# One decoder layer with block-sparse attention and a routed feed-forward: the attention loop issued in source order, and a new order at the start of the last stage

## The chip, the cores and the metric

The kernel runs on one core of one Trainium2 chip. That core has five engines with a queue of instructions each: TensorE (PE: matmuls and transposes; its weight loads are listed as PEld), VectorE (DVE), ScalarE (ACT), GpSimd (POOL) and SyncE (SP, which here only issues DMAs). The metric is the device time of one execution in microseconds, lower is better.

## The reference, cut to what matters

One layer works on h with 1024 tokens of width 1024:

```python
hn = rmsnorm(h)
z  = hn @ w_in                                   # u, v | q | six k/v groups | gates
oa = gelu(u) * (tril(w_s) @ rmsnorm(gelu(v)) + b_s)      # per chunk of 128 tokens
ob = g0*softmax(q kc^T) vc + g1*softmax(q ks^T) vs + g2*softmax(q kw^T) vw
h += concat(rmsnorm(oa), rmsnorm(ob)) @ w_o
h += hier_moe(rmsnorm(h))                        # 16 experts, 2 a token, of one group
h += (p @ w_ple_proj) * sigmoid(rmsnorm(h) @ w_ple_gate)
out = rmsnorm(h)
```

The attention has 8 heads in 2 groups. For the 1024 tokens of this case there are 16 blocks of 64 keys and 16 are selected, so the second branch sees all earlier keys; the third sees the last 512. Everything is float32; the kernel splits most operands into a high and a low part (`hi`, `lo`) and makes three matmuls of each product.

## The kernel before, in words

**Stages.** (1) Normalization and z = hn @ w_in, by column chunks (`z_chunk`). (2) The attention, a generator (`attention`) that walks through 132 slots. (3) `tail`: the last block of tokens, the router. (4) `moe`: 17 fixed blocks of rows with streamed expert weights, and three conditional groups of further blocks. (5) `ple`: gate, projection and the final norm, for eight tiles of 128 rows.

**The attention's slots.** The query blocks are walked in the order 1, 2, 3, 4, 0, 5, 6, 7 (`BLOCKS`). A unit is one block, one head group and one branch; its keys come in chunks of up to 512. A slot is one block of 128 keys of one unit, with 4 heads at once. In slot s the source writes down, in this order: the transposes of the probabilities of slot s+1 (`trans`, L644), their copy `ph` on ACT (L650); what was put off to this slot (`later`, run by `run_later`: exponentials L580, scale factors, copies); `pl` on DVE (L652); the output transposes of a finished group (`out`); steps of the query preparation (`prep`); a number of steps of `work`; the score matmuls of up to two banks into PSUM tiles `S`, of which there are two (L565), each with its maximum on DVE (L570); and the two products with V of slot s (`mult`, L669 and L670). POOL scales the probabilities (L604).

**The filler, `work`.** A second generator gives one matmul a step. In the first part (`z_prod`, tile `u`) it makes the last four row tiles of u, in two pairs of 2 x 24 matmuls, at no fewer than 7 a slot. Behind each pair, in the same step and without a yield, stand the evacuation of both tiles (`evac_u`: L232 on ACT, L244 and L247 on POOL, L245 and L248 on DVE, L246 and L252 on ACT, `rstd` L95 and L96 and L254 on POOL, the store L255 on POOL's queue) and the loading of output weights (`load_wo`: a DMA L745 issued by SP, the high part L748 on POOL, the low part L749 on DVE). Behind the first pair two weight chunks are loaded (2 and 3), behind the second, through `open_late`, four (4 to 7), then `gmoe` and `rt`. The staging tiles of chunks 4 to 7, `hT` and `hg`, have one buffer each. The second part of `work` multiplies by w_o (`prod`, L771), adds to h (`add`), transposes h for the router (`trans_h`) and computes its logits.

The core of the evacuation, one of two tiles whose closures run in the order written:

```python
nc.gpsimd.tensor_tensor(e, x, x, op=OP.mult)
nc.vector.scalar_tensor_tensor(e, e, 1 / 0.044715, x, op0=OP.add, op1=OP.mult)
nc.scalar.activation(e, e, AF.Tanh, scale=math.sqrt(2 / math.pi) * 0.044715)
nc.gpsimd.tensor_tensor(x, x, X[1], op=OP.mult)
nc.vector.scalar_tensor_tensor(x, e, 1.0, x, op0=OP.add, op1=OP.mult)
...
for k in (a, e, b, c, f, d, g, h):
    k()
```

**What sets the order.** Up to and with the attention loop a planner at compile time orders each engine's instructions by priority and by its own estimate of when operands are there; the steps of `work` have low priority there and may not go ahead of the slot's transposes (`issue_after`). From `manual_schedule` on (L1100) each engine gets its instructions in the order in which the source issues them; before, that holds from `tail` on.

**The start of the last stage.** `ple` loads h of tile 0 on SP, and on POOL's queue the two gathered expert outputs of tile 0 (`load_y(0)`, tiles `yg`, L1663), then h and `yg` of tile 1, h of tile 2 and `gf`. `proj(q)` makes a projection of four matmul instructions (L1741); `part(c)` splits one of eight gate weight chunks (ACT L1727, DVE L1728); `add_y(0)` adds the expert outputs (L1671); `trans` and `parts` prepare tile 0 for the gate matmuls (`mult`). The rows that are gathered come from `y_scr`, to which the last MoE block is written at L1613.

Of the kernel before, what the change touches and what calls it, by code (L numbers as in the profile page):

```python
# [8 lines left out]
F32 = mybir.dt.float32  # L9
# [4 lines left out]
AF = mybir.ActivationFunctionType  # L14
# [5 lines left out]
T = 1024  # L20
# [3 lines left out]
NP = 7  # L24
# [48 lines left out]
class K:  # L73
# [328 lines left out]
    def attention(self, blocks, done, work, count):  # L402
# [301 lines left out]
        for s in range(len(slots)):  # L704
            self.now = s
            lo = trans(s + 1) if s + 1 < len(slots) else None
            self.run_later()
            if lo:
                lo()
            for _ in range(min(2, len(self.pq))):  # L710
                self.pq.pop(0)()
            for _ in range(2 - bool(self.pq)):
                for i in [i for i in blocks if at[i] < len(STEPS)][:2]:
                    if start[first[i]] + STEPS[at[i]] - 0 <= s and may_step(i):
                        step(i)
                        break
            left = max(count[0] / (len(slots) - s), 0 if self.late else 7)
            n = 0
            with self.tc.high_priority(offset=-100000), self.tc.issue_after(anchor[0].ins):
                while n < left:  # L720
                    if next(work, None) is None:
                        break
                    count[0] -= 1
                    n += 1
            for n in range(2):
                b = state["bank"]
                if b < len(banks) and (n == 0 or due[b] + 0 <= s) and has_room(banks[b][0]) and may_score(b, due[b] <= s):
                    score()
            evac = mult(s)
            if s == len(slots) - 8:  # L730
                self.ple_load()
# [44 lines left out]
    def work(self, W, blocks):  # L776
# [25 lines left out]
        def load_h(X):  # L802
            X["h1"] = sb.tile([128, T], F32, name="h1", bufs=1)
            nc.sync.dma_start(X["h1"], self.A["x"][0, X["rows"]])
# [20 lines left out]
                nc.sync.dma_start(self.hg_scr[X["rows"]], X["hg"])  # L825

        def rest(X, nxt):
            trans_h(X, 1)
            load_h(nxt)
            self.logits(X["i"], X["hT"], X["hg"][:, T:T + 1])  # L830

        for i, X in M.items():
            X["i"] = i
# [6 lines left out]
        for n, i in enumerate(blocks[:-1]):  # L840
            X, N = M[i], M[blocks[n + 1]]
            X["sq"] = self.small.tile([128, 4], F32, name="sq")

            for t in range(NS + NF + n, NB, len(blocks) - 1):
                nc.sync.dma_start(self.y_scr[t * 128:(t + 1) * 128].rearrange("p (a n) -> p a n", a=2),
                                  X["oa"].unsqueeze(1).to_broadcast([128, 2, 512]))
            load_oa(N)
            while not i in self.ready:
                yield None
            X["ob"] = self.ready[i]  # L850
            trans(X, "ob")
            p = [None, None]
            for k in range(2):
                p[k] = ps.tile([128, 512], F32, name="wo", tag="fl")
                yield from self.prod(p[k], X["toa"], 0, k, True, False)
            trans(N, "oa")
            for k in range(2):
                yield from self.prod(p[k], X["tob"], 1, k, False, True)
                add(X, k, p[k])
                if k == 0:  # L860
                    trans_h(X, 0)
                else:
                    rest(X, N)

        X = M[blocks[-1]]
        for k in range(2):
# [6 lines left out]
    def attended(self, i, ob):  # L873
# [7 lines left out]
        def scale(self=self):  # L881
            sq = self.obs
            self.nc.vector.tensor_scalar(ob, ob, sq[:, 1:2], None, op0=OP.mult)

        def ready():
            self.ready[i] = ob

        norm()
        scale()
        ready()  # L890

    def logits(self, i, hT, scale):
        nc = self.nc
# [33 lines left out]
    def tail(self, att, moe, work, i):  # L927
# [11 lines left out]
        nc.scalar.dma_start(self.c2, self.A["consts2"])  # L939
        self.oh = t[:, 512:1024].bitcast(F16).rearrange("p (k n) -> p k n", k=8)  # L940
        self.moe_start()
        for r in work:
            if r is None:
                self.tick()
        while self.dq or self.pq:
            self.tick()
# [45 lines left out]
    def mixer(self):  # L992
        tc, nc, A = self.tc, self.nc, self.A
        with ExitStack() as st:
# [101 lines left out]
                yield  # L1096

            self.open_late = open_late
            next(att)
            self.manual.enter_context(tc.manual_schedule())  # L1100
            m = self.moe()
            self.tail(att, m, work, blocks[-1])
        for _ in m:
# [253 lines left out]
    def moe(self):  # L1357
# [3 lines left out]
        with ExitStack() as st:  # L1361
# [247 lines left out]
            regs_y.append(B)  # L1609
            AC.activation(o[:, :512], B["y"][0], AF.Copy)  # L1610
            V.tensor_copy(o[:, 512:], B["y"][1])
            for s in (slice(0, 512), slice(512, T)):
                nc.sync.dma_start(self.y_scr[B["t"] * 128:(B["t"] + 1) * 128, s], o[:, s])  # L1613

            with ExitStack() as more:
                for a0, a1 in ((NF, NF + 2), (NF + 2, NF + 5), (NF + 5, 31)):
# [21 lines left out]
    def ple(self):  # L1638
        nc, A = self.nc, self.A
        V, AC, G, PE = nc.vector, nc.scalar, nc.gpsimd, nc.tensor  # L1640
        with ExitStack() as st:
# [77 lines left out]
                    nc.sync.dma_start(self.out[0, X["rows"], s], h[:, s])  # L1719

            load_h(tiles[0], nc.sync)
            W = {}

            def part(c):
# [3 lines left out]
                V.scalar_tensor_tensor(W[c][1], w, g, raw(W[c][0]), op0=OP.mult, op1=OP.subtract)  # L1728

            part(0)  # L1730
            load_y(0)
            pT, pw = self.late_p

            def proj(q):
# [10 lines left out]
                    late.append((X["pe"][:, s], pe))  # L1745

            late = []
            for q in range(4):
                proj(q)
            for c in range(1, 3):  # L1750
                part(c)

            load_h(tiles[1], G)
            load_y(1)
            load_h(tiles[2], G)
            gf = one.tile([128, T], F32, name="gf")
            G.dma_start(gf, A["norm_final"].to_broadcast([128, T]))

            add_y(0)
            trans(tiles[0])  # L1760
            parts(tiles[0])
            for q in range(4, NP):
                proj(q)
            for c in range(3, 8):
                part(c)
                if c in (3, 4, 6):
                    AC.activation(*late.pop(0), AF.Copy)  # L1767
            norm(tiles[0])
            for i, X in enumerate(tiles):
                P = tiles[i - 1] if i else None  # L1770
# [141 lines left out]
```

## Time and profile before

| what | before |
|---|---|
| median of 3 runs (lowest to highest) | 1183.36 us (1180.6 to 1183.68) |
| the profiled execution's own time | 1184.59 us |
| its span, first to last instruction | 1182.9 us |
| PE busy | 1128.9 us, 95% of the span, 5969 matmul instructions |
| DVE, ACT, POOL busy | 761.8, 664.6, 368.5 us (64%, 56%, 31%) |
| mean granted TensorE clock | 0.986 of full speed |

The share of busy time is taken over stages with different limits; the attention lies from about 240 to 620 us, the MoE from about 640 to 1057 us, the last stage behind it. The ends of matmuls are modelled, so that successive matmuls overlap in the rows, and the distance of two starts says what one costs.

### The profile page before, as it was taken

The page shows a single profiled execution, that of the slowest core. Times are in us where ns is not written, and L with a number is a line of the kernel's source. Part 1 is how long each engine was busy: PE and PEld are TensorE (multiplying, and loading weights), DVE is VectorE, ACT ScalarE, POOL GpSimd, SP SyncE. Part 2 cuts the span into 40 slices and gives each one's busy share as a digit, 9 for nine tenths or more (in the row PEclk, how much of TensorE's full clock was granted, in tenths as well). Part 3 has the DMA queues.
Part 4 walks back from the last instruction along what each step waited for, and adds up shares of the span by engine and source line. Part 5 has one row for each costly group of instructions (what it writes and reads, how often), then busy time and mean ns, then how long its engine had stood idle before and what let it go on. Part 6 is the DMA issues. An engine that isn't in the chain of part 4 may idle for free. (4 is left out here: it accounts for less than half of the span.)

```text
span 1182.9 us, 17701 instructions
## 1 busy us (share of the span) xinstructions
PE 1128.9 (95%) x5969; PEld 862.6 (73%) x5969; DVE 761.8 (64%) x1264; ACT 664.6 (56%) x1295; POOL 368.5 (31%) x566
## 2 busy tenths in 40 slices
PE   7999999899899999999999989999999999997996
PEld 5798778777688888887775566766667776655885
DVE  4461144467877687767756568876777787646764
ACT  5562154467577777675643357665675665444433
POOL 1562242357533534433321120121112110012542
PEclk9999999999899999999999999999999999998999
DMA  7685241422530311330257797799768994674561
GB/s 271 203 214 145 66 136 59 155 70 69 192 125 5 108 63 42 98 116 5 79 200 257 290 333 252 248 366 416 284 217 293 410 362 162 197 273 171 187 215 70
DMA packets 75839, 219.54 MB, mean 186 GB/s; under 512 B 12777, under 2 KB 20329, under 8 KB 71137
## 3 DMA queue, kind: packets, MB, share of 16 engines
q1 hardware_dynamic: 63200, 177.68, 43.1%
q0 software_dynamic: 7792, 27.77, 7.4%
q10 hardware_dynamic: 4752, 12.93, 2.8%
q8 instruction: 48, 0.79, 0.3%
q14 instruction: 47, 0.38, 0.1%
HBM read 247.44 MB, written 40.11 MB: 243 GB/s over the span
## 5 line engine op out<-in xcount | busy, mean ns | idle before, releaser
L1413 DVE TENSOR_TENSOR wl<-ra,wh 128x1024 fp32r<-128x1024 f32 x192 | 232.1, 1237 | 54.6 <-ACT wh L1412 38.9
L1412 ACT ACTIVATE wh<-ra 128x1024 fp32r<-128x1024 f32 x176 | 180.3, 1056 | 68.5 <-PE y L91 41.0
L265 PE MATMUL z<-w,xh 128*128 128x512 f32 (+1 forms) x576 | 171.1, 379 | 8.1 <-ACT w L84 7.7
L604 POOL TENSOR_SCALAR P<-P,f 128x384 f32<-128x384 f32 (+3 forms) x188 | 105.1, 579 | 104.9 <-DVE f L625 61.9
L580 ACT ACTIVATE P<-S,nm 128x256 f32<-128x256 f32 (+3 forms) x192 | 105.3, 555 | 48.3 <-DVE nm L570 44.5
L265 PEld LDWEIGHTS z<-w,xh 128*128 128x128 f32 x576 | 105.1, 190 | 27.3 <-ACT w L84 7.7
L652 DVE TENSOR_TENSOR pl<-tp,ph 128x512 fp32r<-128x512 f32 x132 | 89.8, 685 | 39.0 <-ACT ph L650 38.3
L1410 POOL TENSOR_SCALAR wh<-ra 128x1024 fp32r<-128x1024 f32 x16 | 23.7, 1482 | 287.7 <-PE y L91 277.2
L89 PE MATMUL gu<-wh,mxh 128*128 128x512 f32 x256 | 108.3, 423 | 4.8 <-ACT wh L1412 4.8
L570 DVE TENSOR_REDUCE nm<-S 128x1 f32<-128x384 f32 (+3 forms) x148 | 91.6, 627 | 30.7 <-PE S L569 18.1
L265 PE MATMUL z<-w,xl 128*128 128x512 f32 (+1 forms) x288 | 109.0, 379 | 0.9 <-DVE xl L82 0.9
L90 PE MATMUL gu<-wl,mxh 128*128 128x512 f32 x256 | 101.7, 397 | 1.5 <-DVE wl L1413 1.5
L650 ACT ACTIVATE ph<-tp 128x512 fp32r<-128x512 f32 x132 | 78.2, 600 | 42.8 <-PE tp L644 42.2
L91 PE MATMUL gu<-wh,mxl 128*128 128x512 f32 x256 | 101.6, 397 | 0.0
L565 PE MATMUL S<-kT,qT 128*128 128x384 f32 (+3 forms) x384 | 92.6, 349 | 8.8 <-ACT P L580 6.6
L771 PE MATMUL wo<-wo,th 128*128 128x512 f32 x256 | 90.1, 425 | 0.0
L644 PE MATMUL tp<-c,P 128*128 128x128 f32 x528 | 83.5, 275 | 0.4 <-POOL P L604 0.4
L565 PEld LDWEIGHTS S<-kT,qT 128*128 128x128 f32 x384 | 62.9, 195 | 18.6 <-ACT P L580 9.4
L644 PEld LDWEIGHTS tp<-c,P 128*128 128x128 f32 x528 | 65.5, 142 | 12.3 <-POOL P L604 0.7
L89 PEld LDWEIGHTS gu<-wh,mxh 128*128 128x128 f32 x256 | 48.6, 190 | 30.0 <-ACT wh L1412 15.6
L265 PEld LDWEIGHTS z<-w,xl 128*128 128x128 f32 x288 | 54.7, 190 | 11.2 <-DVE xl L82 2.1
L670 PE MATMUL O<-pl,V 128*128 128x512 f32 x132 | 57.1, 433 | 1.0 <-DVE pl L652 1.0
(371 smaller groups left out, 2393.7 us busy)
## 6 DMA issues: line engine op xcount, KB each, us to landing
ra<-in_moe_w_gate SPq DMA_DIRECT2D x32, 1024.0 KB
ra<-in_moe_w_up SPq DMA_DIRECT2D x32, 1024.0 KB
ra<-in_moe_w_down SPq DMA_DIRECT2D x32, 1024.0 KB
rq<-in_moe_w_gate SPq DMA_DIRECT2D x40, 512.0 KB
rq<-in_moe_w_up SPq DMA_DIRECT2D x40, 512.0 KB
rq<-in_moe_w_down SPq DMA_DIRECT2D x40, 512.0 KB
y_scr<-yo ACTq DMA_DIRECT2D x19, 512.0 KB
wraw<-in_w_in SPq DMA_DIRECT2D x32, 256.0 KB
```

The source lines that it names most:

```text
L89: mm(out, xh, wh, start=first, stop=False)
L90: mm(out, xh, wl, start=False, stop=False)
L91: mm(out, xl, wh, start=False, stop=last)
L265: self.nc.tensor.matmul(p[:, :n], x, w, start=(cc == 0 and j == 0), stop=(cc == 7 and j == 2))
L565: PE.matmul(S[:, x], qT[i, g][:, h0 + x, a], kk, start=(x + a == 0), stop=(x == hp - 1 and a == 1 and not (dm or wm)))
L570: V.tensor_reduce(u["nm"][:, h0:h0 + hp, k], S, axis=AX.X, op=OP.max, negate=True)
L580: AC.activation(u["P"][k][:, h], S[:, x], AF.Exp, bias=u["nm"][:, h, k:k + 1], accum_out=u["l"][:, h, k:k + 1])
L604: e.tensor_scalar(P, P, f[:, h, k:k + 1], 1.0, op0=OP.mult, op1=OP.mult)
L644: anchor[0] = PE.transpose(tp[:, h], u["P"][k][:, h, kb * 128:(kb + 1) * 128], self.idf)
L771: self.nc.tensor.matmul(p, x, w[:, s], start=first and k + a == 0, stop=last and k == 3 and a == 2)
L1412: AC.activation(hi, w, AF.Copy)
L1413: V.tensor_tensor(lo, w, raw(hi), op=OP.subtract)
```

## The change

It has three parts. (a) `manual_schedule` begins ahead of the attention loop, so that every engine gets the attention and `work` in the source's order; the low priority and the `issue_after` around the steps of `work` are gone. (b) Some steps are put off by one or two slots with `later`: the transposes of h and the logits, the scaling of a finished block's output and its release; in `tail` the clock of put-off steps advances at every third step of `work` as well. (c) The last block's rows are written to `y_scr` by one DMA on ACT's queue in place of two on SP's. In `ple`, `load_y(0)` stands directly behind the first load; all seven projections stand in one run with `part(1)` to `part(4)` and three copies of projections between them, `add_y(0)` behind the fourth; and POOL first copies a column of the second gathered tile, before it issues the loads for tiles 1 and 2.

```diff
--- before.py
+++ after.py
@@ -716,12 +716,11 @@
                         break
             left = max(count[0] / (len(slots) - s), 0 if self.late else 7)
             n = 0
-            with self.tc.high_priority(offset=-100000), self.tc.issue_after(anchor[0].ins):
-                while n < left:
-                    if next(work, None) is None:
-                        break
-                    count[0] -= 1
-                    n += 1
+            while n < left:
+                if next(work, None) is None:
+                    break
+                count[0] -= 1
+                n += 1
             for n in range(2):
                 b = state["bank"]
                 if b < len(banks) and (n == 0 or due[b] + 0 <= s) and has_room(banks[b][0]) and may_score(b, due[b] <= s):
@@ -825,9 +824,11 @@
                 nc.sync.dma_start(self.hg_scr[X["rows"]], X["hg"])
 
         def rest(X, nxt):
-            trans_h(X, 1)
-            load_h(nxt)
-            self.logits(X["i"], X["hT"], X["hg"][:, T:T + 1])
+            def one():
+                trans_h(X, 1)
+                load_h(nxt)
+
+            return one, lambda: self.logits(X["i"], X["hT"], X["hg"][:, T:T + 1])
 
         for i, X in M.items():
             X["i"] = i
@@ -857,10 +858,11 @@
             for k in range(2):
                 yield from self.prod(p[k], X["tob"], 1, k, False, True)
                 add(X, k, p[k])
+
                 if k == 0:
-                    trans_h(X, 0)
+                    self.later(1, lambda X=X: trans_h(X, 0))
                 else:
-                    rest(X, N)
+                    self.later(1, *rest(X, N))
 
         X = M[blocks[-1]]
         for k in range(2):
@@ -886,8 +888,7 @@
             self.ready[i] = ob
 
         norm()
-        scale()
-        ready()
+        self.later(1, scale, ready)
 
     def logits(self, i, hT, scale):
         nc = self.nc
@@ -939,8 +940,8 @@
         nc.scalar.dma_start(self.c2, self.A["consts2"])
         self.oh = t[:, 512:1024].bitcast(F16).rearrange("p (k n) -> p k n", k=8)
         self.moe_start()
-        for r in work:
-            if r is None:
+        for k, r in enumerate(work):
+            if r is None or k % 3 == 2:
                 self.tick()
         while self.dq or self.pq:
             self.tick()
@@ -1096,8 +1097,8 @@
                 yield
 
             self.open_late = open_late
+            self.manual.enter_context(tc.manual_schedule())
             next(att)
-            self.manual.enter_context(tc.manual_schedule())
             m = self.moe()
             self.tail(att, m, work, blocks[-1])
         for _ in m:
@@ -1609,8 +1610,7 @@
             regs_y.append(B)
             AC.activation(o[:, :512], B["y"][0], AF.Copy)
             V.tensor_copy(o[:, 512:], B["y"][1])
-            for s in (slice(0, 512), slice(512, T)):
-                nc.sync.dma_start(self.y_scr[B["t"] * 128:(B["t"] + 1) * 128, s], o[:, s])
+            nc.scalar.dma_start(self.y_scr[B["t"] * 128:(B["t"] + 1) * 128], o)
 
             with ExitStack() as more:
                 for a0, a1 in ((NF, NF + 2), (NF + 2, NF + 5), (NF + 5, 31)):
@@ -1719,6 +1719,7 @@
                     nc.sync.dma_start(self.out[0, X["rows"], s], h[:, s])
 
             load_h(tiles[0], nc.sync)
+            load_y(0)
             W = {}
 
             def part(c):
@@ -1728,7 +1729,6 @@
                 V.scalar_tensor_tensor(W[c][1], w, g, raw(W[c][0]), op0=OP.mult, op1=OP.subtract)
 
             part(0)
-            load_y(0)
             pT, pw = self.late_p
 
             def proj(q):
@@ -1745,26 +1745,26 @@
                     late.append((X["pe"][:, s], pe))
 
             late = []
-            for q in range(4):
+            for q in range(NP):
                 proj(q)
-            for c in range(1, 3):
-                part(c)
-
+
+                if q < 4:
+                    part(q + 1)
+                if q >= 4:
+                    AC.activation(*late.pop(0), AF.Copy)
+                if q == 3:
+                    add_y(0)
+            trans(tiles[0])
+
+            G.tensor_copy(sb.tile([128, 8], F32, name="sq")[:, 0:1], tiles[0]["y"][1][:, 0:1])
             load_h(tiles[1], G)
             load_y(1)
             load_h(tiles[2], G)
             gf = one.tile([128, T], F32, name="gf")
             G.dma_start(gf, A["norm_final"].to_broadcast([128, T]))
-
-            add_y(0)
-            trans(tiles[0])
             parts(tiles[0])
-            for q in range(4, NP):
-                proj(q)
-            for c in range(3, 8):
+            for c in range(5, 8):
                 part(c)
-                if c in (3, 4, 6):
-                    AC.activation(*late.pop(0), AF.Copy)
             norm(tiles[0])
             for i, X in enumerate(tiles):
                 P = tiles[i - 1] if i else None
```

## Rows read from the trace of the kernel before

**Rows 1.** Windows of the attention: busy us of each engine, granted clock, DMA share, GB/s

```profile
240.00:295.00 55.00, 54.02 (x315) 43.94 (x315) 40.28 (x74) 36.67 (x96) 36.04 (x57) 0.98 0.20 61
295.00:311.00 16.00, 12.57 (x59) 8.73 (x59) 12.09 (x23) 9.59 (x24) 11.50 (x17) 0.79 0.68 218
311.00:600.00 289.00, 287.56 (x1826) 240.64 (x1824) 212.00 (x448) 197.41 (x530) 116.59 (x196) 1.00 0.24 77
```

**Rows 2.** The slots' transposes on PE: duration min/median/max, first and last start

```profile
L644 PE MATMUL tp<-c,P x528: 270/272/473, 239.7 to 614.7; 128*128 128x128 f32 x176
```

**Rows 3.** POOL's groups from 240 to 311 us: busy, mean ns, idle before

```profile
L748 POOL TENSOR_SCALAR wo<-wraw,par 128x512 fp32r<-128x512 f32 x8 | 5.5, 695 | 2.5 <-DMA wraw<-in_w_o 2.5
L247 POOL TENSOR_TENSOR ev<-ev,M 128x512 f32<-128x512 f32 x4 | 5.2, 1290 | 5.1 <-DVE e L245 5.1
L244 POOL TENSOR_TENSOR e<-ev 128x512 f32<-128x512 f32 x4 | 4.2, 1038 | 0.9 <-ACT ev L232 0.9
L254 POOL TENSOR_SCALAR ev<-ev,sv 128x512 f32<-128x512 f32 x4 | 2.8, 692 | 0.4
L255 POOL DMA_DIRECT2D oa_scr<-ev x4 | 2.4, 612 | 0.9 <-POOL ev L254 0.9
L96 POOL TENSOR_TENSOR sv<-sv,neg_half 128x1 f32<-128x1 f32 x4 | 2.2, 554 | 0.3
```

**Rows 4.** DVE's groups from 240 to 311 us

```profile
L570 DVE TENSOR_REDUCE nm<-S 128x1 f32<-128x384 f32 (+2 forms) x29 | 17.3, 611 | 4.7 <-PE S L569 4.4
...
L248 DVE SCALAR_TENSOR_TENSOR ev<-e,ev 128x512 f32<-128x512 f32 x4 | 3.1, 775 | 0.1
L245 DVE SCALAR_TENSOR_TENSOR e<-e,ev 128x512 f32<-128x512 f32 x4 | 2.7, 682 | 0.0
```

**Rows 5.** ACT's groups from 240 to 311 us

```profile
L580 ACT ACTIVATE P<-S,nm 128x384 f32<-128x384 f32 (+2 forms) x33 | 18.6, 569 | 9.8 <-DVE nm L570 9.8
...
L232 ACT ACTIVATE ev<-u,r 128x512 f32<-128x512 f32 x4 | 2.8, 689 | 0.3 <-POOL P L604 0.2
L252 ACT ACTIVATE jk<-ev 128x512 bf16<-128x512 f32 x4 | 2.5, 637 | 3.2 <-DVE ev L248 3.2
```

**Rows 6.** Timeline of one reload of a staging tile, 319 to 325 us

```profile
320.06 0.33 SPq L745 DMA_DIRECT2D hT<-in_w_o  x1
...
322.60 0.69 POOL L748 TENSOR_SCALAR wo<-hT,par 128x512 fp32r<-128x512 f32 x1 [3.68 <-DMA hT<-in_w_o]
323.33 0.75 DVE L749 SCALAR_TENSOR_TENSOR wo<-hT,par,wo 128x512 fp32r<-128x512 f32 x1
324.11 0.33 SPq L745 DMA_DIRECT2D hT<-in_w_o  x1
```

**Rows 7.** The chain that ended last, at the start of the last stage

```profile
1058.41 7.11 PE pe L1741 x16
1065.52 5.02 issue
1070.54 1.94 PE tp L1680 x8
...
1085.24 1.07 PE tp L1680 x8
1086.31 0.23 PE pg L89
```

**Rows 8.** Timeline of DVE and POOL at the start of the last stage

```profile
1062.09 1.01 POOL L1663 DMA_INDIRECT yg<-y_scr,slot  x1 [25.82 <-SPq L1615]
1062.54 3.68 DVE L1728 SCALAR_TENSOR_TENSOR pgl<-rb,par,pgh 128x1024 fp32r<-128x1024 f32 x3 [4.29 <-ACT pgh L1727]
...
1064.64 0.60 POOL L1650 DMA_DIRECT2D h<-h_scr  x1
...
1068.29 2.81 DVE L1671 SCALAR_TENSOR_TENSOR h<-yg,wt,h 128x512 f32<-128x512 f32 x4 [2.07 <-DMA yg<-y_scr,slot]
...
1082.49 1.28 DVE L1671 SCALAR_TENSOR_TENSOR h<-yg,wt,h 128x1024 f32<-128x1024 f32 x1
```

## The prediction

> **What bounds the kernel now.** I read the windows of the attention first, then the groups of instructions by engine there, the timeline of one reload, and at the end the chain that ended last. The windows are to show that TensorE is the limit of the attention: from 311 to 600 us it is busy 287.56 of 289.00 us at full granted clock, with DVE at 212.00 and ACT at 197.41 [rows 1]. So reordering can give back only what PE loses, and each us in which PE stands is lost for good, since no later stretch has slack to catch up. What PE loses: 1.0 us from 240 to 295 (55.00 less 54.02), 3.4 us from 295 to 311 (16.00 less 12.57), and there the granted clock is 0.79, which costs some 0.21 x 16 = 3.4 us more; then 1.4 us in 289 [rows 1]. That is 9.2 us, the most that the first part of the change can win. The transposes of the 132 slots (528, four a slot) start between 239.7 and 614.7, so a slot takes 375 / 132 = 2.84 us [rows 2].
>
> **The attention in source order.** Removed are the low priority and the tie of the filler to the slot's transposes; moved is every instruction of `work` on all engines, its SP and POOL DMAs too, into the place where the source writes it. What matters is what stands there in one piece. `work` yields only at matmuls. At 7 a slot its 48 products of the first pair end in slot 6, those of the second in slot 13, and in the same step the source writes the evacuation of two tiles and the loading of weights, on ACT, DVE, POOL and SP. Behind all that, in each queue, comes what the attention needs next: DVE's maxima of the scores of this very slot, `pl` of the next, ACT's exponentials, POOL's scaling. Before, the planner could put these in between the links of the chain.
>
> Now the chain, worked out with the durations of [rows 3 to 5]. One tile: copy of u 0.69 (ACT), square 1.04 (POOL), DVE 0.68, product with M 1.29 (POOL, which waits for that DVE step: 5.1 us in three of four cases; the tanh beside it is of the size of ACT's 0.64 and shorter), DVE 0.78, square sum 0.64 (ACT), power 0.55, scaling 0.69, store 0.61 (all POOL). That is 7.0 us. The second tile starts on POOL behind the first one's store, so it adds the same without the copy, 6.3 us. Together 13.3 us, with nothing for handing over; POOL's stores alone stood 0.9 / 4 = 0.23 us each for it [rows 3], and at some 17 handings of about 0.1 I take 15 us.
>
> Then the weights, one queue after the other. A half chunk is a high part on POOL and a low part on DVE, and the staging tile is free for the next DMA when DVE has read it: POOL starts at 322.60, DVE ends at 324.08, SP issues the next one at 324.11 [rows 6]. From issue to POOL's start another took 320.06 to 322.60, 2.54 us, in which POOL stood [rows 6]. So a chunk costs 1.51 + 2.54 = 4.05 us, and the last one 0.69 + 2 x 0.75 = 2.2 us. Behind the first pair there are two chunks: 4.05 + 2.2 = 6.3 us. Behind the second there are four: 3 x 4.05 + 2.2 = 14.4 us (`rt`, last in DVE's row, has landed by then, as it is issued right behind the last weights).
>
> So from the last product of a pair until DVE is back at the attention's maxima: 15 + 6.3 = 21.3 us in the first case, 15 + 14.4 = 29.4 us in the second. With a maximum (0.61) and an exponential (0.57) [rows 4, 5] the next score bank is free after 22.5 and 30.6 us. How far does PE get meanwhile? There are two score banks and the next `ph` is behind ACT's part of the chain, so it goes on to the third score, about two slots, 5.7 us [rows 2]; in the second case the filler's next product wants a low part that DVE makes behind the weights, so about one slot, 2.8 us. **The two stalls: 22.5 - 5.7 = 16.8 us and 30.6 - 2.8 = 27.8 us, 44.6 us.**
>
> After 3.4 us of idle time the clock was granted at 0.79 over the 16 us around it, a loss of 3.4 us [rows 1]. Behind each stall I take 2.5 us of the same kind, 5 us in all. Against it, the 3.4 us of idle time and 3.4 us of clock that the old order loses at 295 to 311 go: the same work, now inside the second stall. **Attention: 44.6 + 5 - 6.8 = +42.8 us.** Bounds: from below, no handing over (13.3 us a pair) and three slots of run-ahead in the first case and two in the second, no clock loss, all 9.2 us won: 13.3 + 6.3 + 1.2 - 8.5 = 12.3 and 13.3 + 14.4 + 1.2 - 5.7 = 23.2, less 9.2, is +26. From above, 17 us a pair, one slot of run-ahead both times, 3.4 us of clock each, nothing won: 21.7 + 29.8 + 6.8 = +58. The bounds don't hold the case that nothing stalls; that is a rival.
>
> A rule speaks against this part too: the Trainium skill, "PSUM — Partial Sum Buffer", section "Engine vs sequencer instructions", says that the queues of ScalarE, VectorE and GpSimd are strict first in, first out. The trace agrees: POOL stood 3.68 us for a DMA at 322.60 [rows 6]. By the rule nothing passes a waiting instruction, which is the sum above; an engine that could pass it would give the 9.2 us and no stall.
>
> **The steps put off.** `scale` and `ready`, the transposes of h, and the logits come a slot or two later, so that an in-order queue doesn't stand for them; eight blocks, seven with the filler. Each hides behind the rest of its slot (2.84 us), and block n+1's products need them a dozen slots on. I cost them at nothing; uncovered, each would cost PE about one copy on ACT, like that of u (0.69 us [rows 5]), some 5 us over seven blocks. Their DMAs (`hg_scr`, the load of the next h) go out on SP a slot later, ahead of nothing that is needed in that slot. The tail's more frequent tick: nothing, within 1 us either way.
>
> **The last stage.** Here PE stands 5.02 us, from 1065.52 to 1070.54 [rows 7], until the gathered rows are added to h; then come three projections, and only then the gate products. The gathers' issue at 1062.09 is no earlier after the change, because POOL has nothing else ahead of it; it waits for SP behind the conditional blocks [rows 8]. What does change: the three projections (12 instructions at 7.11 / 16 = 0.44, 5.3 us [rows 7]) fill the wait. DVE makes five parts instead of three (3.68 / 3 = 1.23 each) and is free at 1062.54 + 5 x 1.23 = 1068.7; the rows were there at 1068.29 and the sum takes 2.81 [rows 8], so transposes move from 1070.54 to about 1071, with no idle clock loss before them, and the first gate product to about 1073. Before, the second tile's transposes stood at 1085.24 [rows 7], behind its sum, which starts at 1082.49 and takes 2 x 1.28 [rows 8]. After, DVE is through with its last part at about 1078 (copies until 1073.7, then three parts of 1.23), and tile 1's rows, which POOL now asks for at about 1069.7 instead of 1064.64, must have landed. The load of h takes POOL 0.6 us and a gather some 1.3 (two from 1062.09 to 1064.64), so the second gather is issued at about 1071.9; the first one of tile 0 took 1068.29 - 1062.09 = 6.2 us to be there, so 1078.1. The sum starts at about 1078.0 and ends at 1080.6 instead of 1085.05: 4.4 us won, and all later tiles follow. The write of the last rows as one DMA starts when both halves are there, at the time of the second of the old ones; 0.2 us later to land, from nothing to 0.5. **Last stage: -4.2 us**; bounds 0 (the delayed loads eat it) and -5 (all idle time).
>
> **Sum.** 42.8 - 4.2 = +38.6 us on the profiled execution's own 1184.59: 1223.2. That execution is 1.2 us above the median of the runs, so I predict 1222.0 against 1183.36.
>
> **The rivals.**
>
> Faster: nothing stalls. PE's own run-ahead, or fewer filler instructions in one piece than I count, would hide the chain. It decides if DVE is back within two slots, 5.7 us, of the pair's last product; I count 21 and 29. Then up to 9.2 us are won in the attention and 4.2 in the end: 1170 to 1179. For it speaks that the old order loses 6.8 us exactly where the filler hands over [rows 1]; against it, that POOL's waits in that chain are in the trace even with the planner [rows 3]. Chance 0.16.
>
> Only the evacuations stall, because the weights have long landed and their staging does not hold: 16 - 5.7 and 16 - 2.8 and 3 of clock, where 16 is the chain with a maximum and an exponential, less 6.8 and 4.2, is +15.5: about 1199. POOL's waits for `hT` [rows 6] speak against it. Chance 0.12.
>
> In addition every other slot waits a little, since DVE and ACT are at 73% and 68% of the time [rows 1] and can no longer take what is ready: 0.2 us in 118 slots is 24 us more, 1246 at the most likely sum. Against it, the source staggers exponentials and maxima by a slot. Chance 0.08.
>
> No change that can be measured (within 0.3%, 3.5 us, about what a measurement can tell): one small stall that the last stage pays for. Chance 0.04.
>
> **How the numbers follow.** The two stalls as worked out have 0.60, with a range of their own of 1205 to 1237 (+26 and +58 with the last stage's -4.2 and the 1.2). With the stall of the evacuations and the waits of all slots, slower has 0.80; faster 0.16, the same 0.04. The range must leave out no more than 2 in 10: without the faster case (0.16) and the upper half of the last rival (0.04) it goes from 1184 to 1246.
>
> **What would show it.** Right: in the profile after, two stretches at slots 7 and 14 in which PE is idle for over 10 and over 20 us, S waiting for ACT's exponentials, these for DVE's maxima, and DVE for POOL's evacuation and weights; a granted clock below 1 behind each; POOL's wait for `hT` of some 2.5 us three times in a row. At the end, no 5 us of idle PE ahead of the first transposes, and the second tile's transposes 3 to 4 us nearer to the first gather. Wrong: the transposes of the slots keep their 2.84 us through slots 6 to 16; then the faster rival holds. If PE is near 98% busy there but the slots are longer, the third one holds.

## The result and the profile after

The changed kernel takes 1342.62 us in the median of 4 runs (1341.07 to 1347.16), the kernel before beside it 1183.52: 1.135 times as long, interval 1.1318 to 1.1381. The prediction had the sign and the two stalls, but 1222.0 us. The profiled execution spans 1340.8 us; before it was 1182.9, so it is 157.9 longer.

First the whole attention after in one window, with the columns of [rows 1], and then the slots' transposes, which answer to [rows 2].

```profile
238.00:790.00 552.00, 436.58 (x2344) 346.74 (x2344) 279.12 (x569) 256.04 (x674) 170.69 (x281) 0.86 0.21 69
```

```profile
L644 PE MATMUL tp<-c,P x528: 270/272/476, 238.6 to 767.8; 128*128 128x128 f32 x176
```

The 528 transposes now take 529.2 us from first to last start instead of 375.0, and their median is the same 272 ns. TensorE does the same work, and stands 115.4 of 552 us; the granted clock there is 0.86, where it was 0.98 and more in all of [rows 1] but one short stretch.

Where the time lies, from the starts of the slots' transposes and of the stages (us before | after): slots 0 to 6 27.4 | 30.9, **slots 7 to 16 48.1 | 99.3, slots 17 to 130 299.2 | 398.8**, from the last slot's last transposes to the MoE's first product 33.3 | 40.7, MoE 409.1 | 407.6, from its last product to the second tile's transposes in the last stage 28.1 | 23.9, from there to the end 97.6 | 100.7. So +51.2 stands where the prediction put its two stalls, +99.5 behind them where it put nothing, and +7.4 in the tail.

**The two stalls.** PE's timeline of after (start, duration, line, operation, and in brackets the idle time ahead and who ended it):

```profile
276.01 0.63 PE L265 MATMUL u<-w,xh 128*128 128x512 f32 x2
295.58 1.01 PE L565 MATMUL S<-kT,qT 128*128 128x384 f32 x2 [18.95 <-ACT P L580]
...
327.02 1.09 PE L754 MATMUL tp<-c,oa 128*128 128x128 f32 x4 [8.26 <-DMA oa<-oa_scr]
...
332.84 1.22 PE L770 MATMUL wo<-wo,th 128*128 128x512 f32 x2 [3.88 <-ACT th L81]
...
354.32 0.79 PE L770 MATMUL wo<-wo,tl 128*128 128x512 f32 x1 [13.78 <-DVE tl L82]
```

18.95 us in one piece, then 8.26 + 3.88 + 13.78 = 25.92: together 44.9 us idle, where 44.6 were forecast. What TensorE waits for is named by DVE's timeline of the second one:

```profile
321.54 0.69 DVE L245 SCALAR_TENSOR_TENSOR e<-e,ev 128x512 f32<-128x512 f32 x1 [3.22 <-POOL e L244]
...
328.78 0.69 DVE L245 SCALAR_TENSOR_TENSOR e<-e,ev 128x512 f32<-128x512 f32 x1 [4.48 <-POOL e L244]
...
335.71 1.17 DVE L748 SCALAR_TENSOR_TENSOR wo<-hT,par,wo 128x512 fp32r<-128x512 f32 x1 [4.16 <-POOL wo L747]
...
340.70 0.75 DVE L748 SCALAR_TENSOR_TENSOR wo<-hT,par,wo 128x512 fp32r<-128x512 f32 x1 [3.16 <-POOL wo L747]
...
353.58 1.28 DVE L82 TENSOR_TENSOR tl<-tp,th 128x512 fp32r<-128x512 f32 x2
354.78 0.68 DVE L570 TENSOR_REDUCE nm<-S 128x1 f32<-128x512 f32 x1
```

and by POOL's, which answers to the reload of [rows 6]:

```profile
339.97 0.69 POOL L747 TENSOR_SCALAR wo<-hT,par 128x512 fp32r<-128x512 f32 x1 [3.64 <-DMA hT<-in_w_o]
...
344.11 0.69 POOL L747 TENSOR_SCALAR wo<-hT,par 128x512 fp32r<-128x512 f32 x1 [2.19 <-DMA hT<-in_w_o]
...
348.41 0.69 POOL L747 TENSOR_SCALAR wo<-hT,par 128x512 fp32r<-128x512 f32 x1 [2.06 <-DMA hT<-in_w_o]
```

DVE goes from the evacuations straight to the weights and comes back to a maximum at 354.78, 33 us after its first link. Now the same stretches as windows, with the granted clock:

```profile
276.70:295.50 18.80, 0.00 (x0) 0.00 (x0) 5.88 (x9) 2.48 (x7) 9.57 (x14) 0.61 0.32 107
295.50:300.50 5.00, 4.92 (x15) 3.83 (x16) 1.88 (x5) 3.21 (x9) 2.27 (x4) 0.50 0.00 0
300.50:316.00 15.50, 15.50 (x83) 12.17 (x82) 7.39 (x15) 5.93 (x16) 3.03 (x6) 0.97 0.01 1
318.80:354.30 35.50, 9.64 (x36) 7.97 (x36) 10.08 (x15) 6.43 (x14) 14.80 (x20) 0.54 0.40 128
354.30:369.50 15.20, 11.38 (x37) 8.08 (x37) 7.63 (x15) 3.76 (x8) 3.32 (x5) 0.61 0.23 87
369.50:411.00 41.50, 37.59 (x216) 28.40 (x215) 25.17 (x49) 25.46 (x61) 13.06 (x20) 1.00 0.00 1
```

After the first stall PE works 5 us at 0.50, the lower of its two levels (1.2 GHz): 2.5 us lost. In the second it works in bits, 9.64 us up to 354.3 and 11.38 behind, at 0.54 and 0.61; half of these 21 us, some 10, is an estimate of what that costs.

**Behind the stalls** about half of the loss stands at the ends of blocks. Waits of ACT from 238 to 790 us (total, times, longest):

```profile
ACT ph L650 <- PE tp L644: 164.8, 113, 6.7
ACT P L580 <- DVE nm L570: 36.5, 16, 18.0
ACT jk L822 <- DMA y_scr<-oa: 30.4, 6, 6.3
```

The first row was 42.2 us before. The timeline of the first of the six waits of `jk`:

```profile
411.88 1.26 SPq L846 DMA_DIRECT2D y_scr<-oa  x2
...
418.60 1.06 ACT L822 ACTIVATE jk<-h 128x1024 bf16<-128x1024 f32 x1 [5.06 <-DMA y_scr<-oa]
...
419.66 0.46 ACT L580 ACTIVATE P<-S,nm 128x256 f32<-128x256 f32 x1
...
420.71 1.01 PE L565 MATMUL S<-kT,qT 128*128 128x384 f32 x2 [6.18 <-ACT P L580]
```

`jk` is the output of the square sum in `trans_h`, which nobody reads. It takes a buffer of the ring of `oa`, whose last rows two writes of 512 KB are just sending to `y_scr` as padding for the MoE. ACT stands 5.06 us for a buffer, the next exponential is right behind it in its queue, and behind that PE's next score. Slot 30, where this is, takes 10.8 us instead of 3.3, and slots 47, 63, 79, 94 and 110, where the other five stand, are 6.8 to 13.1 us longer than before, 51.8 us in the six. Slots 72 and 95, without such a wait, are 7.1 and 6.7 us longer.

**The last stage**, which answers to [rows 7, 8]:

```profile
1227.85 2.74 DVE L1671 SCALAR_TENSOR_TENSOR h<-yg,wt,h 128x512 f32<-128x512 f32 x4
1229.08 0.23 POOL L1759 COPY sq<-yg 128x1 f32<-128x1 f32 x1 [5.20 <-DMA yg<-y_scr,slot]
...
1229.98 1.32 PE L1680 MATMUL tp<-c,h 128*128 128x128 f32 x8 [0.28 <-DVE h L1671]
1230.45 1.00 POOL L1663 DMA_INDIRECT yg<-y_scr,slot  x1 [0.30 <-issue]
...
1231.75 0.95 POOL L1663 DMA_INDIRECT yg<-y_scr,slot  x1 [0.30 <-issue]
```

and the chain that ended last, for tile 1:

```profile
1231.75 6.75 DMA yg<-y_scr,slot
...
1238.59 1.30 DVE h L1671
...
1240.02 1.91 PE tp L1680 x8
1241.93 0.43 PE pg L89
```

The 5.02 us of [rows 7] are gone, and tile 1's transposes stand 23.9 us behind the MoE instead of 28.1. There PE waits 2.49 us for the sum with the gathered rows (before, 1.03), and the products behind run at 0.43 us each instead of 0.23 until about 1243.4: the granted clock is 0.66 from 1240 to 1245, and was 1.00 from 1085.2 to 1090 before. That is 1.7 of the 3.1 us by which the rest of the stage is longer.

### The profile page after: what moved, and what is told of

Read it like the earlier page. It is cut to its first block, busy times and chain, and to the rows that moved or that the text cites. A ratio compares the mean times of both kernels' runs of the same rounds, so it can differ in the third digit from the quotient of the medians.

```text
span 1340.8 us, 17696 instructions
## 1 busy us (share of the span) xinstructions
PE 1181.9 (88%) x5969; PEld 893.6 (67%) x5969; DVE 762.2 (57%) x1264; ACT 665.7 (50%) x1295; POOL 368.3 (27%) x567
## 5 line engine op out<-in xcount | busy, mean ns | idle before, releaser
L650 ACT ACTIVATE ph<-tp 128x512 fp32r<-128x512 f32 x132 | 78.7, 597 | 165.2 <-PE tp L644 164.8
L565 PE MATMUL S<-kT,qT 128*128 128x384 f32 (+3 forms) x384 | 100.2, 371 | 60.6 <-ACT P L580 57.9
L604 POOL TENSOR_SCALAR P<-P,f 128x256 f32<-128x256 f32 (+3 forms) x188 | 103.7, 573 | 154.6 <-DVE f L625 95.5
L565 PEld LDWEIGHTS S<-kT,qT 128*128 128x128 f32 x384 | 68.9, 211 | 84.0 <-ACT P L580 71.4
L770 PE MATMUL wo<-wo,th 128*128 128x512 f32 x256 | 95.9, 455 | 3.9 <-ACT th L81 3.9
L644 PEld LDWEIGHTS tp<-c,P 128*128 128x128 f32 x528 | 70.7, 149 | 22.8 <-POOL P L604 3.3
L770 PE MATMUL wo<-wo,tl 128*128 128x512 f32 x128 | 53.1, 415 | 13.8 <-DVE tl L82 13.8
L669 PE MATMUL O<-ph,V 128*128 128x512 f32 x132 | 63.1, 478 | 0.0
```

Of the source, the lines that this page charges most:

```text
L565: PE.matmul(S[:, x], qT[i, g][:, h0 + x, a], kk, start=(x + a == 0), stop=(x == hp - 1 and a == 1 and not (dm or wm)))
L604: e.tensor_scalar(P, P, f[:, h, k:k + 1], 1.0, op0=OP.mult, op1=OP.mult)
L644: anchor[0] = PE.transpose(tp[:, h], u["P"][k][:, h, kb * 128:(kb + 1) * 128], self.idf)
L770: self.nc.tensor.matmul(p, x, w[:, s], start=first and k + a == 0, stop=last and k == 3 and a == 2)
```

## The experiments

All medians are of 4 or more runs; the kernel before took 1182.7 to 1184.5 us beside them. "Planned" is the order that the planner made before, "fixed" the source's.

**Which part costs.** One kernel has the attention of after and the last stage and the write to `y_scr` of before, the other is the reverse.

> Parts (a) and (b) alone: the attention in source order with the steps put off; the write of the last MoE rows and the last stage as before. Theory 1 (all of the loss is made between the first slot and the end of the tail): 1340 to 1347 us, since the trace after puts 154 us of 158 between the first and the last slot and 7.5 us into the tail. Rival (the last stage loses several us too): below 1338.

> Part (c) alone, with the attention of before. The prediction's own term: 4.2 us faster, 1179.3. From the trace after, where the second tile's transposes stand 4.3 us nearer to the last expert matmul but the rest of the stage takes 3.1 us longer: 1 to 2.5 us faster, 1181 to 1182.5. Rival (the delayed loads eat it): 1183 or more.

att_only 1347.73 us (ratio 1.1347 to 1.1399), 0.7 above the range that I expected; ple_only 1179.09 (0.9943 to 0.9971). All of the loss is in the attention and its tail. The last stage gains 4.6 us by the medians, where its term in the prediction was 4.2 and I had expected less from the trace. In ple_only's one profile the same stretch as above is 23.1 us instead of 28.1, and 100.7 instead of 97.6 come behind it: the stage as a whole gains only 1.9 us there, so the traces don't show where the rest of the 4.6 is won.

**The shared buffer.** Only the output of the square sum gets a ring of its own:

```diff
-AC.activation(sb.tile([128, T], BF, name="jk", tag="oa", bufs=2), X["h1"], AF.Square, accum_out=X["sq"][:, 0:1])
+AC.activation(self.sb.tile([128, T], BF, name="jk", tag="ph"), X["h1"], AF.Square, accum_out=X["sq"][:, 0:1])
```

> The kernel after, but the square sum of a finished block writes its unused output to a tile of the ph ring instead of the ring of oa, which two pad writes to y_scr may still be reading. Theory 1 (in one fixed queue ACT's waits for these writes, 30.4 us in six places, hold the scores, and SP's loads of q stand behind them): 30 to 60 us less than after, 1283 to 1313. Rival 2 (the loss is spread: every slot loses a little to in-order handing over, wherever one looks): at most 10 us less, above 1330.

1292.52 us (1.0892 to 1.094): 50.1 us less than after. Its timeline where after had the wait:

```profile
409.16 2.97 SPq L846 DMA_DIRECT2D y_scr<-oa  x2
...
410.72 1.06 ACT L822 ACTIVATE jk<-h 128x1024 bf16<-128x1024 f32 x1
...
412.83 0.62 PE L565 MATMUL S<-kT,qT 128*128 128x384 f32 x2 [1.02 <-ACT P L580]
```

The square sum no longer waits for the writes. Slots 17 to 130 go from 398.8 to 351.5 us (-47.3), slots 7 to 16 from 99.3 only to 95.8: the buffer's price lies where the stalls do not. In slots 17 to 130 TensorE's idle time falls by 25.5 us and its busy time by 21.8 with the same 1906 matmuls, as the granted clock goes from 0.91 to 0.98.

**The two chains.** The evacuations and the weights are written link by link over the slots, two links a slot (`c`, `d`, `g` and `h` yield behind each link; the second pair does so inside `work`), with two empty steps ahead of the first product with w_o:

```diff
-            for k in (a, e, b, c, f, d, g, h):
-                k()
+            a(), e(), b()
+
+            def links():
+                yield from c()
+                f()
+                yield from d()
+                yield from g()
+                yield from h()
...
+                for j in range(7):
+                    self.later(1 + j, lambda links=links: (next(links, None), next(links, None)))
+                for j, q in enumerate(range(2 * t2 - 2, 2 * t2)):
+                    self.load_wo(q, self.sb, "xs", at=4 * j)
```

> The kernel after, but the evacuations of u and the output weights are written out link by link: two links of an evacuation a slot, the high and low part of a weight chunk one or two slots behind its DMA. Theory 1 (the two chains written in one piece stop DVE, ACT and POOL): the two stretches with 19 and 30 us of idle PE and 8 and 22 us of lost clock go, 45 to 80 us less, 1262 to 1298. Rival 2 (spread loss): 0 to 20 us less, above 1322.

> Both edits of jk_own and split on the kernel after. Theory 1: the savings add, 80 to 130 us less than after, 1212 to 1262, and the granted clock of the attention is above 0.95. Rival 2 (spread loss in every slot): above 1300.

split took 1305.96 us (1.1018 to 1.1059), 36.7 less than after and below what I expected; split_jk, with both edits, 1266.06 (1.0677 to 1.0734), 76.6 less, just short of the 80 that I expected at least, with a granted clock of 0.94 in the attention. In split, slots 7 to 16 take 52.9 us instead of 99.3, so all but 4.8 us of what the stalls cost is gone; slots 17 to 130 take 406.4 instead of 398.8, where links and weights now stand. The two causes nearly add (36.7 + 50.1 = 86.8), and 83 us over before are still there.

**The order itself, and queue by queue.** In no_manual, `manual_schedule` begins behind the attention again, with all else as in after. In the others, one or some queues of the attention are fixed:

```diff
-            self.manual.enter_context(tc.manual_schedule())
-            next(att)
+            with tc.manual_schedule(engines={...}):
+                next(att)
+            self.manual.enter_context(tc.manual_schedule())
```

> The kernel after, but the fixed order begins behind the attention, as before; the filler has no low priority and the steps stay put off. Theory 1 (fixing the order is the cause): 1178 to 1195. Rival 3 (the lost low priority of the filler, or the steps put off, cost most of it): above 1230.

> The kernel after, but in the attention only TensorE's instructions keep the source's order; the other four engines are planned. Theory 1 (the chains stand in the queues of DVE, ACT, POOL and SP): most of the loss goes, 1185 to 1240. Rival 4 (TensorE itself, with the filler's matmuls ahead of the scores, makes the loss): above 1290.

> The reverse: ACT, DVE, POOL and SP keep the source's order in the attention, TensorE is planned. Theory 1: 1270 to 1340. Rival 4: below 1240.

> As the changed kernel, but in the attention only ACT keeps the source's order; PE, DVE, POOL and SP are ordered by the planner. All queues planned gave 1192.3, TensorE alone fixed 1210.4, the other four fixed 1304.2. Theory (what costs is ACT and DVE in turn: ACT stands at a copy that waits for TensorE while an exponential behind it could run, and DVE stands for ACT): ACT alone gives a large part, 1220 to 1270. Rival (the chain of evacuation and weights and the square sum's buffer cost only where all queues stand together): ACT alone stays within 15 us of 1192, as the others' planner fits itself around it.

> As the changed kernel, but in the attention only DVE keeps the source's order. Theory (DVE is the queue in which the low parts of the weights and the evacuation's steps stand ahead of the maxima): 1215 to 1260. Rival (only queues that stand together cost): within 15 us of 1192.

> As the changed kernel, but in the attention only POOL and SP keep the source's order. Theory (POOL has slack, 31% busy, and SP only issues DMAs, so their order costs little unless POOL's scaling of the probabilities stands behind the evacuation): 1192 to 1215. Rival (POOL's and SP's waits for DMAs carry the loss): above 1230.

| fixed in the attention | us | ratio to before, interval | over no_manual |
|---|---|---|---|
| none (no_manual) | 1192.29 | 1.0045 to 1.0103 | |
| PE (man_pe) | 1210.39 | 1.0196 to 1.0253 | 18.1 |
| POOL and SP (man_queues) | 1220.67 | 1.0255 to 1.0347 | 28.4 |
| ACT (man_act) | 1236.27 | 1.0362 to 1.0473 | 44.0 |
| DVE (man_dve) | 1281.74 | 1.0769 to 1.0851 | 89.5 |
| all but PE (man_rest) | 1304.19 | 1.0998 to 1.1068 | 111.9 |
| all (after) | 1342.62 | 1.1318 to 1.1381 | 150.3 |

So the fixed order costs 150.3 us over the same kernel planned. DVE alone makes more than half of them, more than I expected of it; POOL with SP costs more than the 1215 of my theory and less than the 1230 of its rival. The price lies in different places: against no_manual, slots 7 to 16 go from 41.2 to 90.8 us with DVE fixed, to 76.1 with POOL and SP and to 56.9 with ACT, and slots 17 to 130 from 306.2 to 331.2, 298.2 and 343.2. As far as slots can be compared (the planner moves filler between them), DVE's and POOL's orders cost most at the chains, ACT's behind them. DVE's timeline in man_dve, where POOL and ACT were free to go around:

```profile
281.88 0.68 DVE L245 SCALAR_TENSOR_TENSOR e<-e,ev 128x512 f32<-128x512 f32 x1
284.66 0.69 DVE L248 SCALAR_TENSOR_TENSOR ev<-e,ev 128x512 f32<-128x512 f32 x1 [2.10 <-POOL ev L247]
288.07 0.69 DVE L245 SCALAR_TENSOR_TENSOR e<-e,ev 128x512 f32<-128x512 f32 x1 [2.72 <-POOL e L244]
290.60 0.69 DVE L248 SCALAR_TENSOR_TENSOR ev<-e,ev 128x512 f32<-128x512 f32 x1 [1.84 <-POOL ev L247]
291.21 1.41 DVE L748 SCALAR_TENSOR_TENSOR wo<-wraw,par,wo 128x512 fp32r<-128x512 f32 x2
297.23 1.53 DVE L748 SCALAR_TENSOR_TENSOR wo<-wraw,par,wo 128x512 fp32r<-128x512 f32 x1 [4.61 <-POOL wo L747]
```

No maximum and no `pl` stands between these rows: the chain holds up the attention through DVE's queue, whatever the other queues do. Slots 7 to 16 take 90.8 us there, almost the 99.3 of after. TensorE had written the next scores by 283.0 us, and their maximum starts at 300.02, behind the chain. The rule weighed in the prediction (the Trainium skill, "PSUM — Partial Sum Buffer", "Engine vs sequencer instructions": strict first in, first out) agrees with this: in the 2.10, 2.72, 1.84 and 4.61 us in which DVE stood above, nothing from behind went ahead.

**What is left in split_jk.** The same edit on split_jk, with one queue (or two, or all) planned again:

> The kernel split_jk (chains spread over the slots, the square sum's output in a buffer of its own), but DVE's queue in the attention is ordered by the planner; PE, ACT, POOL and SP keep the source's order. split_jk gave 1266.1. Theory (what is left is still mostly DVE's order, which alone cost 89 us in the unsplit kernel): 1200 to 1230. Rival (DVE's share was the long chains, which split_jk has spread; what is left is small waits on every queue in turn): 1240 to 1262.

> As split_jk, but ACT's queue in the attention is ordered by the planner. Theory (DVE's order carries most of what is left): 1245 to 1266. Rival (ACT's does, since it stands 156 us at copies of transposes that wait for TensorE, in front of exponentials that could run): 1205 to 1235. Small waits on every queue in turn: 1240 to 1260.

> As split_jk, but TensorE's queue in the attention is ordered by the planner. Theory: TensorE's order alone cost 18 us in the unsplit kernel, so 1240 to 1260. Rival (TensorE is the queue that turns each small wait into idle time, since a filler product behind a waiting score can't go ahead): 1195 to 1235.

> As split_jk, but DVE's and ACT's queues in the attention are ordered by the planner; PE, POOL and SP keep the source's order. split_jk gave 1266.1; DVE planned alone saved 33.7, ACT alone 19.4. If their orders cost separately: 1205 to 1220. If each of the two has only shifted the same waits to the other: 1225 to 1235, no better than DVE alone. If the two pass each wait on (both must be free for either to gain): below 1200.

> As split_jk, but every queue in the attention is ordered by the planner: the price of the edits of split_jk themselves, without any fixed order. The same for the changed kernel (no_manual) gave 1192.3. Theory (the edits themselves cost nothing): 1185 to 1197. Rival (spreading the chains makes the filler's own rows late and costs even with a planner): 1200 to 1225, and then that much of what is left in split_jk isn't the order's.

| planned in split_jk | us | ratio to before, interval | under split_jk |
|---|---|---|---|
| PE | 1268.37 | 1.0682 to 1.0755 | -2.3 |
| ACT | 1246.67 | 1.0485 to 1.0573 | 19.4 |
| DVE | 1232.42 | 1.0375 to 1.0446 | 33.6 |
| DVE and ACT | 1210.14 | 1.019 to 1.0251 | 55.9 |
| all | 1195.27 | 1.0078 to 1.0125 | 70.8 |

DVE's and ACT's orders nearly add up (33.6 + 19.4 = 53.0 against 55.9), though DVE planned came 2.4 us above the range of my theory; PE, POOL and SP together hold 14.9, and TensorE planned alone gains nothing, against both of my ranges; the edits of split_jk cost 3.0 even planned (1195.27 against 1192.29), and their intervals overlap. What stands in split_jk is many short waits and a few of 5 us; the four largest sums among TensorE's waits from 230 to 740 us:

```profile
PE S L572 <- ACT P L587: 26.0, 24, 4.1
PE tp L774 <- DVE pl L659: 6.7, 2, 5.9
PE O L677 <- DVE pl L659: 6.2, 2, 5.1
PE O L670 <- ACT oe L681: 5.7, 10, 1.4
```

and the first of these rows with DVE and ACT planned, from 238 to 690:

```profile
PE S L572 <- ACT P L587: 6.8, 12, 1.5
```

**The steps put off.** After, with part (b) undone: transposes of h, logits, scaling, release and the tail's clock as before.

```diff
-                    self.later(1, lambda X=X: trans_h(X, 0))
+                    trans_h(X, 0)
...
-                    self.later(1, *rest(X, N))
+                    rest(X, N)
...
-        self.later(1, scale, ready)
+        scale()
+        ready()
```

> As the changed kernel (all engines in the source's order), but the steps that it puts off stand where they stood before: transposes of h, logits, scaling of a finished block, release, and the tail's clock. The prediction costed the putting off at nothing. Theory (in a fixed order it is a help: a step that waits is issued when its operands are there): slower than the changed kernel's 1342.6 by 5 to 40 us. Rival (putting off is itself a cost, because it moves the square sum with the shared buffer and SP's DMAs into slots that need the queues): faster, 1300 to 1335.

1354.68 us (1.1375 to 1.1463), 12.1 more than after. On balance putting off helps in a fixed order; TensorE's waits from 238 to 804 us show with what:

```profile
PE S L565 <- ACT P L580: 34.9, 23, 19.0
PE tp L754 <- DVE h L813: 21.7, 7, 4.4
PE tp L754 <- issue: 14.6, 7, 2.3
```

Without it TensorE stands seven times for the sum h at the transposes. But the square sum does not wait at all there, as its row says, with nothing listed as idle time ahead of any of the seven:

```profile
L822 ACT ACTIVATE jk<-h x7: 1048/1048/1049, 420.0 to 777.6; 128x1024 bf16<-128x1024 f32 x7
its engine sat idle before it (us, times) until:
who waited for it (us, times):
  POOL hg L95: 7.8, 6
```

The reason is in the source. Not put off, the square sum stands ahead of the next block's padding writes and takes the buffer whose own writes are long done; put off by a slot, it stands right behind these writes and takes the buffer that they read. So part (b) is a gain and a loss in one: slots 17 to 130 take 420.2 us without it, 398.8 with it, and 351.5 with it and a buffer of the square sum's own. The tail is 32.1 us there, not 40.7: of the edits in part (b), those that reach the tail cost some 8 us.

**A faster version.** ple_only beats both kernels. With the square sum's own buffer as well:

> The kernel before with the new order of the last stage (ple_only, 1179.1) and the square sum's output in a buffer of its own. Before, TensorE lost 8.4 us of idle time in the attention and the planner had put most waits elsewhere. Theory: the shared buffer costs a planned order next to nothing, 1176 to 1181. Rival: it holds up part of the blocks' ends there as well, 1168 to 1175.

1181.61 us (0.9967 to 1.0004): no gain over ple_only, and 0.6 above the range that I expected. There the square sum is not put off. Where it is put off and planned, in no_manual, it does not wait for the writes either, and a buffer of its own gains nothing (sj_all_planned, with it and the chains spread, takes 3.0 us more). In a planned order the shared buffer costs nothing that shows.

## Why the prediction was wrong

**What bounds the kernel: right.** With TensorE at the limit, next to no idle us came back: of the attention's loss the MoE behind it made up 1.5.

**The two stalls: right in place and cause; that the size agrees is partly luck.** 44.9 us idle against 44.6, at slots 8 and 14 to 15, DVE standing for POOL's evacuation and weights, POOL three times for `hT`. The shares came out otherwise: 18.95 and 25.92 against 16.8 and 27.8. DVE was back at the maxima 36.0 us behind the second pair's last product, not 29.4, and a chunk took 4.1 to 5.0 us instead of 4.05; against that TensorE worked 9.64 us between its waits, where the prediction gave it 2.8. The first of these waits was one that it had not foreseen: its next product was the transposes of the rows that had just been stored (8.26 us for `oa`).

**The clock behind them: mis-sized.** 5 us were taken. The first stall cost the 2.5 us forecast; the second, in which TensorE worked in bits between waits, some 10. With that estimate slots 7 to 16 come to 44.9 + 12.5 - 6.8 = 50.6, and +51.2 was measured against +42.8.

**"I cost them at nothing; uncovered, ... some 5 us over seven blocks": the step that failed first.** I looked for the wait in the operands of the steps put off, and not in their output. The square sum's unused output waits for a buffer from which DMAs read; jk_own shows 50.1 us for it. It takes both parts of the change: in the same fixed order but not put off, the square sum never waits (not_put_off), and put off but planned it does not either (no_manual). not_put_off is 12.1 us slower than after and 62.2 slower than jk_own, so putting off gains more than the buffer takes; I had put both at nothing.

**The third rival, "every other slot waits a little", came true in addition, and I gave it 0.08 and 0.2 us.** It is 52.3 us in slots 17 to 130 of jk_own, without the buffer's share: 0.46 us a slot in the mean of 114. It is not even: by groups of six slots it goes from -3.4 to +10.1 us. TensorE is idle 31.9 us there in 49 waits, none over 2 us, against 1.6 us of idle time before; the rest is longer busy time. In split_jk, with the links spread over them, it is 371.7 - 299.2 = 72.5. My argument against it, that the source staggers exponentials and maxima by a slot, did not hold: planning DVE and ACT again gives 55.9 us back. That it follows from DVE and ACT standing for each other in turn (ACT 164.8 us for the transposes ahead of `ph`, in 113 waits) is my reading; the runs show whose order costs, not each wait.

**The tail "within 1 us": wrong**, +7.4, and without part (b) it is not longer than before (32.1 against 33.3).

**The last stage: right in what moves; the size is borne out by the medians alone.** -4.6 was timed against -4.2, and the second tile's transposes are 4.2 us nearer in the profile of after. But "all later tiles follow" did not hold: 3.1 us are given back behind them, some of it by the clock, for which the prediction had no term there. Its 0.2 us for the single write came from no row, and no run shows them by themselves.

**The rivals "nothing stalls" and "only the evacuations stall"** fall with the timelines above.

The sum, from medians, in the order in which the causes were taken away: the buffer and the two chains 76.6 together (50.1 and 36.7 alone), the order of DVE and ACT in what is left 55.9, of the other queues 14.9, split_jk's edits 3.0: these make the 150.3 (the last digit by rounding). no_manual is 13.2 over ple_only: lost priority and steps put off, in a planned order. The last stage takes 4.6 off. What stays open: which of the two makes the 13.2, how the 14.9 divide, and where the last stage loses what the clock does not explain of the 3.1 us.

## What to carry to other kernels

Before a planner's order is replaced by the source's, list for each queue what the source writes in one piece: here a chain over several engines that cost 6.8 us as low-priority filler held up every engine that it passed, and DVE, the busiest elementwise queue, most. For every instruction of a fixed order ask not only when its operands are there but when its output buffer is free; an output that nobody reads still waited here for the DMAs that read its buffer, and it did so because putting the step off had moved it behind them. And measure the parts by themselves: here a part that gains 4.6 us was hidden under one that loses 164.

## What the chip showed that I had not expected

TensorE's granted clock was low for longer behind idle time than the prediction took it: 0.61 in the 18.8 us in which it did nothing, 0.50 in the 5 us of full work behind, 0.97 in the 15.5 us after that; where it works in bits (9.64 us of 35.5) it stays at 0.54, and it was at 0.61 for another 15 us with 11.38 us of work. Over the whole attention it was 0.86. So here a wait was paid twice where the work behind it had further waits in it.
